# A hybrid decoder on one core: the mixer takes two heads with both token halves at a time

## The chip, the cores and the metric

The kernel runs on one core of a Trainium2 chip. The metric is device time in microseconds (us) of one execution. The engines are called as the profile calls them: PE multiplies matrices (PEld is its weight load), DVE and ACT work on tiles element by element, POOL does the same more slowly, and SP issues nearly all DMAs.

## The reference: what is computed

Two layers over 1024 tokens with 1024 channels, all in float32. Each layer is a mixer and an FFN (feed-forward network), each with a residual. The core of the mixer, cut:

```python
h = rms_norm(x, norm1_g)
proj = h @ w_in                      # 1024 x 3592: q, k, v, z (4 heads of 128 each), b, a, 3 x 512 for the short convolution
qkv = silu(causal_depthwise_conv(qkv, dn_conv_w))       # 4 taps
q, k = l2_normalize(q), l2_normalize(k)
beta = sigmoid(b_in); g = -exp(dn_a_log) * softplus(a_in + dn_dt_bias)
o_dn = chunk_gated_delta_rule(q, k, v, g, beta)          # a state of 128 x 128 per head, carried over the tokens
o_dn = rms(o_dn) * dn_norm_g * silu(z)
y = gate_b * causal_depthwise_conv(gate_c * hv, sc_conv_w)   # 3 taps
o_sc = rms(y) * sc_norm_g
x = x + concatenate([o_dn, o_sc]) @ w_out
x = x + (silu(h2 @ ffn_w_gate) * (h2 @ ffn_w_up)) @ ffn_w_down   # h2 = rms_norm(x, norm2_g), 2816 wide
```

The delta rule works chunk by chunk: inside a chunk a unit triangular matrix is inverted, between chunks the state S is carried on.

## The kernel before, in words

Tiles are 128 channels by 512 tokens, one half of the tokens; chunks are 128 tokens, so a half has four. Float32 is emulated: each operand is split into a rounded part `hi` and a rest `lo`, and a product is three matmuls, hi by hi, lo by hi and hi by lo (`mm3`, L176 to L181). One projection of 128 columns for one half is 8 times 3 matmuls of 128x512.

Weights come in tiles of 1024 by 128 (512 KB). `split_w` (L163) loads one, then `split_raw` casts it on ACT to `hi` (L172) and subtracts on DVE to get `lo` (L173). The input projection has 28 such tiles per layer, and the kernel works through the halves one after the other, so each tile is loaded and split twice per layer.

For one half the mixer runs: `make_h` (the normed input as hi/lo tiles), `ba` (beta and the decays of this half), then for each of four heads `proj_kvq` and `prep`; `invert` for the four heads; `chain` for the four heads; `sconv` for four groups, `sc_norm`, `zproj` and `gate`. One head with one half is called a unit below: three projections (72 matmuls of 128x512), each with `conv_silu` (L397: ACT copies the projection out of PSUM, DVE takes four taps at L408 and L410, ACT takes a tanh, DVE combines at L413), then 12 PE transposes (`ktok`, `qtok`, `vtok`), and 8 products `gk` and `gq` that are two passes each, 28 short PE records in all. `prep` computes row sums of squares (ACT L429, DVE L430), an inverse square root by ten small DVE operations (L151 to L160), decay rows `row` (ACT L464), and `U` and `A` on DVE, four operations of 128x128 each (L500).

`invert` is a loop of 31 steps on DVE over 32x32 blocks of all units at once, followed by merges on PE (`rp32`, `yp32`, `rp64`, `yp64`). `chain` carries the state: per chunk kS (PE), rr (DVE), TR (PE), vn (DVE), SU (PE), S (DVE), each needing the one before; each head is alone in its chain.

The second half's input x waits in DRAM (`xd`): `x_half1` puts it there during the first half of layer 0, and each mixer reads it back.

What sets the order: every engine runs its own instructions strictly in the order of the program, and a scheduler puts them into that order when the kernel is built. SP's queue is one such order. A pool gives a tile a fixed number of buffers: four for weight parts `whi` and `wlo`, three for the raw tiles. Where two tiles share a buffer, the later one waits for the last reader of the earlier one.

The FFN uses a scheme with 7 products instead of 8 for 2x2 blocks (`QORD`, P1 to P7); its operands go through the same rings and through buffers that the mixer also uses.

## Time and profile before

| what | us |
| --- | --- |
| three runs: median, lowest, highest | 2424.56, 2420.68, 2424.63 |
| the profiled execution, its own time | 2427.01 |
| its span, first to last instruction | 2425.3 |
| PE busy | 2344.0, 97% |
| DVE busy | 1821.2, 75% |
| ACT busy | 883.5, 36% |
| POOL busy | 720.5, 30% |

The span is what the engines show; 1.7 us of the execution lie around it. Busy shares are means over stages. The stretch from 0 to 500 us holds the mixer of layer 0, the one from 1200 to 1700 us that of layer 1, the rest are output projections and FFNs. A PE counted as busy may still be working below its pace, because one matmul's record overlaps the next; the number of records in a stretch says more.

### The profile page before, as it was taken

How to read it: one execution, taken by the hardware profiler on the slowest of the kernel's cores; microseconds unless marked ns; L12 is line 12 of the kernel's file. 1: busy time of each engine (PE TensorE's matmuls, PEld its weight loads, DVE VectorE, ACT ScalarE, POOL GpSimd, SP SyncE). 2: the span in 40 equal slices, each digit the busy share in tenths (PEclk: the TensorE clock that was granted, in tenths of full speed). 3: DMA queues.
4: the chain of work that ended last, by engine and by line, in shares of the span. 5: the costliest groups of instructions: out<-in, count | busy, mean ns of one | idle time of the engine just before them, and what ended most of it. 6: DMA issues, size and time to landing. Idle time of an engine off the chain costs nothing.

```text
span 2425.3 us, 32283 instructions
## 1 busy us (share of the span) xinstructions
PE 2344.0 (97%) x11530; PEld 1901.9 (78%) x11530; DVE 1821.2 (75%) x3607; ACT 883.5 (36%) x1389; POOL 720.5 (30%) x554
## 2 busy tenths in 40 slices
PE   8899999999999999999999999999999999999998
PEld 6787778886888888777777877878878888887777
DVE  7986996868566665889789779967686565568994
ACT  4522432434323223433344235334342323333334
POOL 2100100034543443456411000000444343434470
PEclk9999999999999999999999999999999999999999
DMA  7545343751432323745243354447433232346431
GB/s 224 137 107 150 97 112 89 208 180 61 126 113 87 109 94 105 239 143 150 96 127 98 95 148 107 111 120 220 126 91 115 86 113 91 117 138 218 139 119 70
DMA packets 423194, 307.74 MB, mean 127 GB/s; under 512 B 48463, under 2 KB 355961, under 8 KB 423033
## 3 DMA queue, kind: packets, MB, share of 16 engines
q1 hardware_dynamic: 423032, 305.69, 42.8%
q8 instruction: 90, 1.47, 0.3%
q14 instruction: 72, 0.58, 0.1%
HBM read 230.59 MB, written 75.04 MB: 126 GB/s over the span
## 4 chain that ended last, share of the span: by engine, by line
PE 74%; DVE 15%; DMA 6%; issue 2%; POOL 1%; ACT 1%; SPq 0%; POOLq 0%; ACTq 0%; DVEq 0%
PE P_g L180 6%; PE P_g L181 6%; PE P_g L179 6%; PE P_u L180 5%; PE P_u L179 5%; PE P_u L181 5%; PE P_d L180 3%; PE P_d L181 3%; PE P_d L179 3%; PE po L181 2%; PE po L179 2%; PE po L180 2%; DMA stP<-hs_P 1%; DMA row<-gd 1%; PE ps_bsc L181 1%
## 5 line engine op out<-in xcount | busy, mean ns | idle before, releaser
L180 PE MATMUL P_g<-lo_hP,hiP_g 128*128 128x512 f32 x616 | 241.7, 393 | 8.6 <-POOL lo_hP L760 4.7
L179 PE MATMUL P_g<-hi_hP,hiP_g 128*128 128x512 f32 x616 | 240.3, 391 | 1.2 <-ACT hi_hP L759 0.9
L180 PE MATMUL P_u<-lo_hP,hiP_u 128*128 128x512 f32 x616 | 240.9, 391 | 0.0
L181 PE MATMUL P_u<-hi_hP,loP_u 128*128 128x512 f32 x616 | 240.9, 391 | 0.0
L179 PE MATMUL P_u<-hi_hP,hiP_u 128*128 128x512 f32 x616 | 240.8, 391 | 0.0
L181 PE MATMUL P_g<-hi_hP,loP_g 128*128 128x512 f32 x616 | 239.7, 390 | 0.0
L180 PE MATMUL P_d<-lo_dP,hiP_d 128*128 128x512 f32 x504 | 199.5, 396 | 14.9 <-DVE lo_dP L760 13.4
L181 PE MATMUL P_d<-hi_dP,loP_d 128*128 128x512 f32 x504 | 196.7, 390 | 2.6 <-DVE loP_d L785 2.6
L179 PE MATMUL P_d<-hi_dP,hiP_d 128*128 128x512 f32 x504 | 196.4, 390 | 0.0
L180 PEld LDWEIGHTS P_g<-lo_hP,hiP_g 128*128 128x128 f32 x616 | 115.6, 188 | 39.7 <-DVE lo_hP L760 8.6
L784 ACT CAST hiP_g<-m_g 128x1024 fp32r<-128x1024 f32 (+1 forms) x66 | 60.1, 910 | 218.5 <-PE P_u L180 193.0
L760 POOL TENSOR_TENSOR lo_hP<-xh,hi_hP 128x512 fp32r<-128x512 f32 x24 | 38.0, 1614 | 336.2 <-ACT hi_hP L759 336.2
L179 PEld LDWEIGHTS P_g<-hi_hP,hiP_g 128*128 128x128 f32 x616 | 115.5, 188 | 27.3 <-ACT hi_hP L759 3.5
L179 PEld LDWEIGHTS P_u<-hi_hP,hiP_u 128*128 128x128 f32 x616 | 116.5, 189 | 24.4
L180 PEld LDWEIGHTS P_u<-lo_hP,hiP_u 128*128 128x128 f32 x616 | 116.4, 189 | 24.3
L181 PEld LDWEIGHTS P_u<-hi_hP,loP_u 128*128 128x128 f32 x616 | 116.3, 189 | 24.3
L181 PEld LDWEIGHTS P_g<-hi_hP,loP_g 128*128 128x128 f32 x616 | 115.7, 188 | 23.2
L1055 DVE TENSOR_TENSOR xT<-P_d,xT 128x512 f32<-128x512 f32 x192 | 124.9, 679 | 9.3 <-PE P_d L181 8.9
L180 PEld LDWEIGHTS P_d<-lo_dP,hiP_d 128*128 128x128 f32 x504 | 94.6, 188 | 46.5 <-DVE lo_dP L760 22.7
L181 PEld LDWEIGHTS P_d<-hi_dP,loP_d 128*128 128x128 f32 x504 | 94.7, 188 | 22.3 <-DVE loP_d L785 3.9
L179 PEld LDWEIGHTS P_d<-hi_dP,hiP_d 128*128 128x128 f32 x504 | 94.6, 188 | 19.8
L784 ACT CAST hiP_u<-m_u 128x1024 fp32r<-128x1024 f32 (+1 forms) x66 | 59.8, 909 | 136.9 <-PE P_g L180 68.2
(413 smaller groups left out, 6219.6 us busy)
## 6 DMA issues: line engine op xcount, KB each, us to landing
stP<-hs_P SPq DMA_DIRECT2D x126, 256.0 KB, 3.9
m_g<-in_ffn_w_gate_dram SPq DMA_DIRECT2D x44, 512.0 KB, 4.0
m_u<-in_ffn_w_up_dram SPq DMA_DIRECT2D x44, 512.0 KB, 4.6
hs_P<-t SPq DMA_DIRECT2D x72, 256.0 KB, 3.2
m_d<-in_ffn_w_down_dram SPq DMA_DIRECT2D x48, 384.0 KB, 4.0
hs_P<-c_u SPq DMA_DIRECT2D x70, 256.0 KB, 2.1
raw_o<-in_w_out_dram SPq DMA_DIRECT2D x32, 512.0 KB, 4.6
raw_k<-in_w_in_dram SPq DMA_DIRECT2D x16, 512.0 KB, 4.6
```

The costliest lines, as they stand in the source:

```text
L179: PE.matmul(ps, lhsT=w(k)[0], rhs=m(k)[0], start=k == 0, stop=False)
L180: PE.matmul(ps, lhsT=w(k)[0], rhs=m(k)[1], start=False, stop=False)
L181: PE.matmul(ps, lhsT=w(k)[1], rhs=m(k)[0], start=False, stop=k == n - 1)
L760: eng.tensor_tensor(res[1], src, res[0].bitcast(F32), ALU.subtract)
L784: S.copy(hi, src)
L1055: V.tensor_tensor(t, ps, t, ALU.add)
```

## The change

The loop is turned round: `for g in range(2)` takes two heads at a time and both halves of them, and a weight tile stays in its buffer for both halves. For that, the normed input of both halves must exist from the start: in layer 0 the second half of x is loaded and transposed in the prologue and in layer 1 `h1` is made where layer 0 ends. `ba` runs once for both halves. The statistics of a head are one piece of 16 columns (`head_stats`); sums of squares are taken by ACT with its accumulator, in four pieces; the first tap goes to ACT; the factor `c2` is put into `row` on POOL, so that U and A are one DVE operation each; `vn` is an ACT copy; two heads' chains alternate; the scaling of the short convolution moves to the load of the output projection's operands. Weight rings have three buffers instead of four. The matmuls of the projections stay as many as they were.

```diff
-NHB = 20
+NHB = 32
...
-    prep_ = ctx.enter_context(tc.tile_pool(name="prep", bufs=2))
+    prep_ = ctx.enter_context(tc.tile_pool(name="prep", bufs=3))
...
-        hi = ring.tile(list(raw.shape), F32R, tag="whi", name=f"hi_{name}")
-        lo = ring.tile(list(raw.shape), F32R, tag="wlo", name=f"lo_{name}")
+            hi = ring.tile(list(raw.shape), F32R, tag="whi", bufs=3, name=f"hi_{name}")
+            lo = ring.tile(list(raw.shape), F32R, tag="wlo", bufs=3, name=f"lo_{name}")
...
+            dma(xp[c][kk], x[0, HALF + c * P:HALF + (c + 1) * P, kk * HALF:(kk + 1) * HALF])
...
+            S.activation(sq, xp[c][kk], AF.Square, accum_out=s2x[:, c, kk:kk + 1])
+            ps = ps_(XTB[(c * 2 + kk) % 4], f"xtp1_{c}_{kk}", (P, 4, P))
+            for k in range(4):
+                PE.transpose(ps[:, k, :], xp[c][kk][:, k * P:(k + 1) * P], ident)
+            for k in range(4):
+                S.copy(xT[1][kk * 4 + k][:, c * P:(c + 1) * P], ps[:, k, :])
...
+    h1 = make_h(lambda k: xT[1][k], r, lambda k: c_norm1(0, k), ps_("fx", "bc_n1_0_1"), "n1_0_1")
+    for k in range(KD):
+        dma(xd[:, k, HALF:], xT[1][k])
...
-                V.tensor_scalar(y, pre[:, 0:HALF], c_conv(l, 0, chan), None, ALU.mult)
-                for j in range(1, 4):
+                S.activation(y, ps, AF.Copy, scale=c_conv(l, 3, chan))
...
+                for j in range(3):
                     V.scalar_tensor_tensor(y, pre[:, j:j + HALF], c_conv(l, j, chan), y, ALU.mult, ALU.add)
...
-                S.activation(sq, ps, AF.Square)
-                V.reduce_sum(dst, sq, axis=AX.X)
+                for c in range(4):
+                    S.activation(sq[:, c, :], ps[:, c, :], AF.Square, accum_out=dst[:, c:c + 1])
...
+                G.tensor_tensor(row, row, c2.unsqueeze(2).broadcast_to(sh4), ALU.mult)
...
-                    for c in range(4):
-                        V.scalar_tensor_tensor(dst[:, c, :], gp[:, c, :], sc[:, c:c + 1], row[:, c, :],
-                                               ALU.mult, ALU.mult)
+                    V.tensor_tensor(dst, gp, row, ALU.mult)
...
-                    V.tensor_scalar(vn, cp, pr["c1"][:, c:c + 1], None, ALU.mult)
+                        S.copy(vn, cp)
...
-                for g, y in enumerate(ys):
-                    rb = tmp("rb", f"rb_{nm}_{g}")
-                    dma(rb, dram_ap(rd[half], g * HALF, [[0, P], [1, HALF]]))
-                    V.tensor_tensor(y, y, rb, ALU.mult)
-                    dma(od[4 + g][half][:], y)
...
+            for g in range(2):
+                slots = {}
+                for hd in (2 * g, 2 * g + 1):
+                    if hd == 0:
+                        for ty in "kqv":
+                            kvq(hd, 0, ty)
+                        ba()
+                        for ty in "kq":
+                            kvq(hd, 1, ty)
+                    else:
+                        for ty in "kq":
+                            for half in range(2):
+                                kvq(hd, half, ty)
+                    head_stats(hd)
+                    for half in range(2):
+                        if (hd, half) != (0, 0):
+                            kvq(hd, half, "v")
+                        slots[hd, half] = len(slots)
+                        prep(hd, half, slots[hd, half])
+                invert(g)
+                for half in range(2):
+                    for hd in (2 * g, 2 * g + 1):
+                        merge(hd, half, slots[hd, half])
+                for half in range(2):
+                    chain(g, half)
+                if g == 0:
+                    for hd in range(2):
+                        w = split_w(wcols(1536 + hd * P), f"z{l}_{hd}")
+                        for half in range(2):
+                            zproj(hd, half, w)
...
+                    sconv(0)
+            for g in range(1, 4):
+                sconv(g)
+            sc_norm()
+            w = [split_w(wcols(1536 + hd * P), f"z{l}_{hd}") for hd in (2, 3)]
...
+                    if k >= 4:
+                        rb = sb("kdec", f"rb_{nm}_{k}")
+                        dma(rb, dram_ap(rd, ((k - 4) * NC + half * 4) * P, [[0, P], [1, HALF]]))
+                        V.tensor_tensor(ot, ot, rb, ALU.mult)
```

In the diff `V` is DVE, `S` is ACT and `G` is POOL. The new `head_stats` does for both halves of a head what `prep` did for one: the transposes of k and q, the sums of squares into 16 columns, one inverse square root, and the factors from it. In `chain` the loop over the two heads now lies inside the loop over the chunks.

Three places of the order. First SP's queue in the prologue of layer 0, where `wd` are zeroed DRAM buffers, `raw_q0_0_0` is the weight tile of q of head 0 for half 0. Before:

```order
L297 DMA wd0_119<-zero_406 128x4x128
L297 DMA wd1_120<-zero_406 128x4x128
L297 DMA wd2_121<-zero_406 128x4x128
L297 DMA wd3_122<-zero_406 128x4x128
L166 DMA raw_q0_0_0_572<-in_w_in_dram 128x8x128
L166 DMA raw_k0_1_0_725<-in_w_in_dram 128x8x128
L166 DMA raw_v0_1_0_770<-in_w_in_dram 128x8x128
L688 DMA xt1_0_970<-in_x_dram 128x1024
```

Now, with `raw_v0_0` the tile of v of head 0 and `xT1` the transposed tiles of the second half:

```order
L306 DMA xd_92<-xT1_0_243 128x512
L306 DMA xd_92<-xT1_1_244 128x512
L306 DMA xd_92<-xT1_2_245 128x512
L306 DMA xd_92<-xT1_3_246 128x512
L306 DMA xd_92<-xT1_4_247 128x512
L306 DMA xd_92<-xT1_5_248 128x512
L306 DMA xd_92<-xT1_6_249 128x512
L306 DMA xd_92<-xT1_7_250 128x512
L312 DMA wd3_121<-zero_597 128x4x128
L166 DMA raw_v0_0_688<-in_w_in_dram 128x8x128
L166 DMA raw_k0_1_1088<-in_w_in_dram 128x8x128
```

The eight writes of the second half's x to DRAM now stand ahead of the third weight tile; before, only zeros and the first half's writes did.

Second DVE in the projection stage of layer 0, before (end of the unit of head 0, into head 1):

```order
L479 TENSOR_TENSOR kdec_0_0_0_642<-kdec_0_0_0_642,kd_0_0_0_664 128x512
L500 SCALAR_TENSOR_TENSOR U_0_0_0_703<-gk_0_0_0_705,c2_0_0_0_663,row_0_0_0_617 128x128 x4
L500 SCALAR_TENSOR_TENSOR A_0_0_0_704<-gq_0_0_0_714,y_rk0_0_0_648,row_0_0_0_617 128x128 x4
L408 TENSOR_SCALAR y_v0_1_0_807<-pre_v0_1_0_803,cst1_88 128x512
L173 TENSOR_TENSOR lo_q0_2_0_1169<-raw_q0_2_0_1166,hi_q0_2_0_1168 128x1024
L410 SCALAR_TENSOR_TENSOR y_v0_1_0_807<-pre_v0_1_0_803,cst1_88,y_v0_1_0_807 128x512
L460 TENSOR_SCALAR ngl_0_2_0_1216<-gcum0_417 128x4
L173 TENSOR_TENSOR lo_k0_3_0_1322<-raw_k0_3_0_1319,hi_k0_3_0_1321 128x1024
L410 SCALAR_TENSOR_TENSOR y_v0_1_0_807<-pre_v0_1_0_803,cst1_88,y_v0_1_0_807 128x512
L406 COPY haloc1_0_847<-pre_q0_1_0_848 128x3
L408 TENSOR_SCALAR y_q0_1_0_852<-pre_q0_1_0_848,cst1_88 128x512
L410 SCALAR_TENSOR_TENSOR y_v0_1_0_807<-pre_v0_1_0_803,cst1_88,y_v0_1_0_807 128x512
```

Now, between head 2's two halves and head 3:

```order
L514 TENSOR_TENSOR U_0_2_0_2697<-gk_0_2_0_2699,row_0_2_0_2672 128x512
L501 TENSOR_TENSOR kdec_0_2_0_2565<-kdec_0_2_0_2565,kd_0_2_0_2677 128x512
L514 TENSOR_TENSOR A_0_2_0_2698<-gq_0_2_0_2705,row_0_2_0_2672 128x512
L424 SCALAR_TENSOR_TENSOR y_v0_2_1_2742<-pre_v0_2_1_2739,cst1_88,y_v0_2_1_2742 128x512 x3
L427 SCALAR_TENSOR_TENSOR vT_v0_2_1_2738<-pre_v0_2_1_2739,y_v0_2_1_2742 128x512
L492 TENSOR_TENSOR kd_0_2_1_2754<-row_0_2_1_2749,gcum0_608 128x4
L422 COPY halock3_0_2822<-pre_k0_3_0_2823 128x3
L417 COPY pre_k0_3_1_2860<-halock3_0_2822 128x3
L490 COPY gl_0_2_2627<-eta_0_2_1_2751 128x4
L495 TENSOR_TENSOR kd_0_2_1_2754<-kd_0_2_1_2754,c2_0_2_2619 128x4
L501 TENSOR_TENSOR kdec_0_2_1_2587<-kdec_0_2_1_2587,kd_0_2_1_2754 128x512
L504 SCALAR_TENSOR_TENSOR v2_0_2_1_2772<-vtok_0_2_1_2767,irk_0_2_2618 128x512
```

U and A are one operation instead of four, the first tap (L408) is gone, and a weight split (L176 there) is met half as often.

Third PE at the start of the first chain phase of layer 0, where TR, SU, op and kS belong to the chain, `rp32` and `yp32` to the merge of another unit, and `ps_` are projections of 128x512. Before:

```order
L589 MATMUL TR_0_0_0_0_1829<-v2_0_0_0_701,Y_0_0_0_1644 128x128
L180 MATMUL ps_z0_3_0_2734<-hlo_n1_0_0_2_362,hi_z0_3_0_2730 128x512
L181 MATMUL ps_z0_3_0_2734<-hhi_n1_0_0_2_361,lo_z0_3_0_2731 128x512
L179 MATMUL ps_z0_3_0_2734<-hhi_n1_0_0_3_367,hi_z0_3_0_2730 128x512
L594 MATMUL SU_0_0_0_0_1833<-vn_0_0_0_0_1831,kdec_0_0_0_642 128x128
L542 MATMUL rp32_0_1_0_1695<-X_0_1_0_1691,U_0_1_0_946 32x32
L603 MATMUL op_0_0_0_1828<-vn_0_0_0_0_1831,A_0_0_0_704 128x128
L180 MATMUL ps_z0_3_0_2734<-hlo_n1_0_0_3_368,hi_z0_3_0_2730 128x512
L542 MATMUL rp32_0_1_0_1695<-X_0_1_0_1691,U_0_1_0_946 32x32 x7
L181 MATMUL ps_z0_3_0_2734<-hhi_n1_0_0_3_367,lo_z0_3_0_2731 128x512
L179 MATMUL ps_z0_3_0_2734<-hhi_n1_0_0_4_373,hi_z0_3_0_2730 128x512
```

Now:

```order
L183 MATMUL ps_q0_2_0_2485<-hlo_n1_0_0_7_414,hi_q0_2_2481 128x512
L184 MATMUL ps_q0_2_0_2485<-hhi_n1_0_0_7_413,lo_q0_2_2482 128x512
L606 MATMUL TR_0_0_0_0_1747<-v2_0_0_0_993,Y_0_0_0_1561 128x128
L611 MATMUL SU_0_0_0_0_1751<-vn_0_0_0_0_1749,kdec_0_0_0_907 128x128
L621 MATMUL op_0_0_0_1745<-vn_0_0_0_0_1749,A_0_0_0_996 128x128
L601 MATMUL kS_0_0_0_1_1765<-S_0_0_0_0_1753,kT_k0_0_0_637 128x128
L620 MATMUL op_0_0_0_1745<-S_0_0_0_0_1753,qT_q0_0_0_675 128x128
L606 MATMUL TR_0_0_0_1_1769<-rr_0_0_0_1_1767,Y_0_0_0_1561 128x128
L557 MATMUL rp32_0_1_0_1612<-X_0_1_0_1608,U_0_1_0_1386 32x32 x8
L611 MATMUL SU_0_0_0_1_1773<-vn_0_0_0_1_1771,kdec_0_0_0_907 128x128
L621 MATMUL op_0_0_0_1745<-vn_0_0_0_1_1771,A_0_0_0_996 128x128
L565 MATMUL yp32_0_1_0_1624<-Y_0_1_0_1607,R32_0_1_0_1621 32x32 x2
```

Before, projection matmuls stood between the steps of the chain; now the first steps follow one another with only merges between them. Further on, 24 matmuls of `ps_q0_2_1` and the first of `ps_v0_2_0` stand in this phase.

## Rows read from the trace of the kernel before

**Rows 1.** The page, its first part: busy us, share of the span, instructions by engine

```profile
PE 2344.0 (97%) x11530; PEld 1901.9 (78%) x11530; DVE 1821.2 (75%) x3607; ACT 883.5 (36%) x1389; POOL 720.5 (30%) x554
```

**Rows 2.** 50 us of the FFN of layer 0: by engine busy us (xinstructions), PEclk, DMA share, GB/s

```profile
650.00:700.00 50.00, 50.00 (x222) 41.40 (x222) 30.88 (x35) 16.14 (x21) 18.33 (x14) 1.00 0.29 89
```

**Rows 3.** Timeline, head 3's chain in layer 0: start us, us, engine, line, operation

```profile
472.37 0.38 PE L584 MATMUL kS<-S,kT_k 128*128 128x128 f32 x2
...
472.59 0.39 PE L602 MATMUL op<-S,qT_q 128*128 128x128 f32 x2
...
475.58 0.38 PE L584 MATMUL kS<-S,kT_k 128*128 128x128 f32 x2
...
476.59 1.14 ACT L613 ACTIVATE on<-op,mo 128x128 f32<-128x128 f32 x4 [0.97 <-DVE mo L610]
```

**Rows 4.** The view of windows again, projection stages, layer 0, then layer 1

```profile
25.00:125.00 100.00, 92.05 (x451) 73.89 (x450) 86.80 (x263) 51.47 (x103) 13.46 (x23) 0.97 0.57 154
275.00:350.00 75.00, 71.27 (x360) 57.80 (x359) 73.78 (x247) 36.53 (x70) 8.83 (x8) 1.00 0.45 116
1200.00:1325.00 125.00, 119.44 (x583) 95.59 (x582) 114.00 (x327) 58.44 (x101) 22.72 (x27) 0.99 0.39 105
1460.00:1550.00 90.00, 85.81 (x436) 70.11 (x436) 87.67 (x286) 41.17 (x76) 8.85 (x8) 1.00 0.43 112
```

**Rows 5.** What PE waited for, 25 to 125 us: us in total, times, longest

```profile
PE vtok L438 <- DVE vT_v L413: 3.3, 2, 2.1
PE ktok L438 <- DVE kT_k L413: 2.0, 1, 2.0
```

**Rows 6.** DVE's groups, 26 to 125 us: xcount, busy us, mean ns, idle before

```profile
L410 DVE SCALAR_TENSOR_TENSOR y_v<-pre_v,cst,y_v 128x512 f32<-128x512 f32 x12 | 9.0, 747 | 0.1
...
L500 DVE SCALAR_TENSOR_TENSOR U<-gk,c,row 128x128 f32<-128x128 f32 x12 | 3.8, 342 | 0.0
...
L173 DVE TENSOR_TENSOR lo_k<-raw_k,hi_k 128x1024 fp32r<-128x1024 f32 x3 | 3.7, 1220 | 0.0
...
L430 DVE TENSOR_REDUCE sk<-sqk 128x4 f32<-128x512 f32 x4 | 2.7, 675 | 0.0
...
L408 DVE TENSOR_SCALAR y_k<-pre_k,cst 128x512 f32<-128x512 f32 x4 | 1.8, 458 | 0.0
...
L153 DVE TENSOR_SCALAR h_rk<-sk 128x4 f32<-128x4 f32 x3 | 0.5, 162 | 0.0
```

**Rows 7.** ACT's groups of the same stretch

```profile
L464 ACT ACTIVATE row<-row,ngl 128x128 f32<-128x128 f32 x15 | 4.8, 392 | 1.8 <-POOL row L461 1.8
...
L172 ACT CAST hi_v<-raw_v 128x1024 fp32r<-128x1024 f32 x3 | 3.1, 1047 | 2.1 <-DMA raw_v<-in_w_in_dram 2.0
...
L429 ACT ACTIVATE sqk<-kdec 128x512 f32<-128x512 f32 x4 | 2.5, 619 | 0.0
...
L691 ACT ACTIVATION_READ_ACCUMULATOR sq<-xt 128x1 f32 x8 | 1.5, 188 | 0.0
```

**Rows 8.** Timeline, one POOL operation and the DVE operation beside it

```profile
72.11 0.97 POOL L461 TENSOR_SCALAR_AFFINE_SELECT row<-row 128x512 f32<-128x512 f32 x1 [0.69 <-DVE kdx L458]
...
72.50 1.12 DVE L410 SCALAR_TENSOR_TENSOR y_q<-pre_q,cst,y_q 128x512 f32<-128x512 f32 x1
```

**Rows 9.** Timeline of the first 25 us: ACT, PE, SP's queue

```profile
16.86 0.20 ACT L293 ACTIVATE alog<-alog 128x8 f32<-128x8 f32 x1
...
19.57 0.59 PE L333 MATMUL ba_ps<-hhi_n,w_ba 128*16 128x512 f32 x1 [1.58 <-ACT hhi_n L214]
...
13.50 5.22 SPq L291 DMA_DIRECT2D xd<-xT  x8
```

**Rows 10.** DMA issues, 25 to 125 us: xcount, KB each, median us to landing

```profile
raw_q<-in_w_in_dram SPq DMA_DIRECT2D x4, 512.0 KB, 5.4
```

**Rows 11.** Windows of the first two chain phases of layer 0

```profile
202.90:267.20 64.30, 60.03 (x497) 46.80 (x497) 50.11 (x152) 24.42 (x53) 6.04 (x5) 0.97 0.52 140
421.40:477.30 55.90, 55.90 (x489) 45.27 (x489) 44.11 (x128) 25.57 (x48) 0.00 (x0) 1.00 0.70 192
```

More of the change, by code (lines that the diff above doesn't have):

```diff
@@ L125, in tile_hybrid @@
     od = [[dram.tile([P, HALF], F32, name=f"od{k}_{h}") for h in range(2)] for k in range(KD)]
-    gd = [dram.tile([16, P], F32, name=f"gd{h}") for h in range(2)]
+    gd = dram.tile([32, P], F32, name="gd")
     USZ = 129 * 128
@@ new lines, in chain @@
+                        if not first:
+                            PE.matmul(op[hd][:, c, :], lhsT=u["q"][:, cs], rhs=St, start=True, stop=False)
+                        PE.matmul(op[hd][:, c, :], lhsT=u["A"][:, c, :], rhs=vn, start=first, stop=True)
+                nm, h4 = f"{l}_{g}_{half}", slice(half * 4, half * 4 + 4)
+                mo = s8("mo", nm)
+                for i, hd in enumerate(hds):
+                    sumsq(op[hd], mo[:, i * 4:i * 4 + 4], f"o_{nm}_{i}")
+                    V.tensor_tensor(mo[:, i * 4:i * 4 + 4], mo[:, i * 4:i * 4 + 4], units[hd, half]["s2"][:, h4], ALU.mult)
```

602 lines of the change are left out of this document (285 added, 317 removed).

## The prediction

> **What bounds the kernel now.** I read the page first, then the windows, then PE's waits, and last the groups of DVE and ACT. On the page PE is busy 2344.0 of 2425.3 us [rows 1], so it looks as if nothing but matmul work could be taken away, and the change takes none. The windows correct this. In the FFN PE runs 222 matmuls of 128x512 in 50 us [rows 2], 0.225 us each. A short PE pass of 128x128 takes 0.11 us: in the timeline two of them start at 472.37 and the next pair at 472.59 [rows 3]. A unit of the mixer (one head, one half) has 72 of the first and 28 of the second: 72 x 0.225 + 28 x 0.11 = 19.3 us, or 0.193 us per record. Against this the projection stages are slow [rows 4]: 451 records should take 87.0 us and stand in 100, 360 take 69.5 of 75, 583 take 112.5 of 125, 436 take 84.1 of 90. So 13.0 + 5.5 + 12.5 + 5.9 = 36.9 us are lost there, though only 8.0 + 3.7 + 5.6 + 4.2 = 21.4 us of them show as idle PE. The rest is hidden in records that overlap less than they could. (Counting each window in the proportion 72 to 28 is an estimate; the other records there, x transposes and `ba`, are of the same two kinds.)
>
> The cause is to be seen in the same rows: DVE is busy 73.78 of 75 us in the window at 275 and 87.67 of 90 in the one at 1460. Per 100 PE records (one unit) that is 73.78 / 3.60 = 20.5 us of DVE, more than PE's 19.3. And PE's waits name it: the transposes of v and k wait for the convolution results vT and kT of DVE, 3.3 and 2.0 us between 25 and 125 [rows 5].
>
> **The change part by part.**
>
> DVE in a unit. Weight splits: three of 1.22 us [rows 6] per unit become three for two units, 1.83 us less. First taps: three of 0.458, 1.37 us less. Row sums: two of 0.675, 1.35 us less. U and A: eight of 0.342 become two of 128x512, which I price at 0.675 like the reduction of that shape, 1.39 us less. Two inverse square roots of ten small operations (0.162 each) per unit become one for two units: 15 x 0.162 = 2.43 us less. Together 8.4 us of 20.5. Records of an engine overlap a little, so the low end counts the first three alone: 4.6. DVE comes to 12.1 to 15.9 us per unit and is no longer the bound.
>
> ACT in a unit. It has 36.53 us in 3.60 units [rows 4], 10.1 each. Casts of 1.047 [rows 7] halve: -1.57. Two Squares of 0.619 go: -1.24. Three first taps of the same shape come: +1.86. Eight Squares of 128x128 at 0.392 with a read of the accumulator at 0.188 come: +4.64. Sum 13.8 us, still under 19.3. POOL gets one more operation of 128x512 per unit, on top of 8.83 / 3.60 = 2.5 us; the nearest row is its 0.97 [rows 8].
>
> So in the projection stages the unit falls from DVE's pace to PE's. What can be won is between all that is lost, 36.9, and what the two named waits explain: 5.3 of the 13.0 in the first window, which as a share of 36.9 is 15 us. What would stay in the second case is latency: the path from PSUM over ACT, three taps, tanh and the combination to the transposes does not get shorter. I take the middle, 26 us.
>
> Prologue of layer 0. The second half of x is now loaded, squared, transposed and copied there. ACT was free at 17.0 us [rows 9]. Before the last copy it now has 32 copies of 128x128 (four took 1.14 us [rows 3], so 9.1), eight Squares with reads (0.619 + 0.188, 6.5) and the eight casts of the first half's input (priced as 128x512, 0.619, 5.0): about 37.6 us. SP's queue holds the eight writes of those tiles to `xd`, then one zeroing write, then the load of v's first tile. Eight such writes took 5.22 us to issue [rows 9]; whether they go one by one as the tiles are done or all behind the last copy, the load leaves between 38.3 and 43, lands 5.4 us later [rows 10], and its cast adds 1.05: 45 to 49 us. PE's order has that v projection ahead of `ba` and of everything else. PE began the projections at 19.57 [rows 9] and until then has k and q of half 0 (48 x 0.225 = 10.8) and 32 transposes (3.5), done at about 34. It then stands idle for 11 to 15 us, of which 3.5 come back, since those transposes no longer stand in the stage behind. I take +9; the ends are 0 (the writes are out early) and +15.
>
> Chain phases. The two of layer 0 take 64.3 and 55.9 us now, with 4.3 and no us of idle PE [rows 11]. The order shows two changes: fewer projection matmuls stand between the steps (by the order some 115 in the first phase before, some 60 now, 12 us less cover), and two heads alternate, where before each head's chain ran by itself. A step of one head takes 3.21 us when little is in its way (kS at 472.37, the next at 475.58 [rows 3]); eight steps are 26 us. PE's own work in a phase is 60.0 - 115 x 0.225 = 34 us of chain and merge, plus 60 x 0.225 = 13.5, so 47.6: there are 22 us for the merges ahead of the last head's chain. vn goes from DVE to ACT; a 128x128 operation of ACT is 0.29 to 0.39 [rows 3, 7], of DVE 0.34 [rows 6], no difference by itself, but ACT's casts of 1.05 can stand ahead of it. I take 0; the ends are -8.6 (the idle 4.3 of the first phase goes in both layers, since DVE is freer and `make_h` has left the phase) and 8 x 1.05 = 8.4 in each of four phases, +34.
>
> Costed at nothing: the halved weight traffic (28 tiles x 512 KB x 2 layers), as the DMA share is 0.39 to 0.57 and no wait of PE names a weight tile in the stages; the ring of three weight buffers, since a split (1.05 + 1.22 = 2.3 us) fits beside one product of 12 matmuls (2.7 us) and PE is busy 50.00 of 50.00 in the FFN, at most one uncovered split at each of four passages between stages, +9; the second half's input at the start of layer 1, with 88 matmuls (19.8 us) of half 0 ahead of its first reader, against 8 x 0.75 + 4 x 0.68 = 8.7 us of DVE; the scaling in the output projection, where the 16 operations of about 0.68 us only move and z's projections (96 matmuls, 21.6 us) cover the statistics.
>
> One rule speaks against the new POOL work. While POOL worked 0.97 us from 72.11, a tap on DVE that takes 0.747 [rows 6] took 1.12 [rows 8]: DVE was held up 0.37. The Trainium skill, "Perfetto Trace Analysis", section "Optimizing Scalar/DVE Operations", says that GpSimd and DVE share a read port of SBUF, so that moving work between the two may not help; the trace agrees as far as this one row goes. By that rule the new row operation can take back up to its own length of DVE in every unit, and the time would move from the forecast towards rival A. The row alone shows a hold of 0.37 us for 0.97 us of POOL; it leaves DVE's unit under PE's, and so it counts here only in A's chance, which it raises a little.
>
> The sum: the profiled execution, 2427.0, less 26, plus 9, is 2410.0. It lies 2.4 above the median of the runs (2424.56), so I predict 2407.6, rounded 2408.
>
> **Rivals.**
>
> A, the gain is eaten (chance 0.16). Latency, not DVE's load, holds PE's transposes, so only 15 us are won, and the prologue costs its full 15: 2427.0 - 2.4 = 2424.6. For it: named waits are a minority of the lost time, ACT, which now takes both the copy and the first tap, lies on the same path, and POOL, which can hold DVE up [rows 8], has more to do. Against it: DVE had no free time at all at 275, so its queue is a delay of its own.
>
> B, slower (0.14). The chains lose their cover: with PE's order fixed, a late vn holds up both heads and the merges behind it. It decides from a step of about 4.2 us on, one cast more than 3.21; then the four phases cost up to 34, and with the projection gain at 26 and the prologue at 9 the time is 2441.6. With half of it the kernel would be level. For it: PE's order starts the first phase with steps and merges and no projection between. Against it: 47.6 us of PE work against 26 of steps.
>
> C, a larger gain (0.15). All 36.9 are won, the idle 8.6 of the chains too, and the writes in the prologue are out early: 2427.0 - 45.5 - 2.4 = 2379.
>
> **How the numbers follow.** The forecast has 0.55, with a range of its own of 2396 to 2417 (projections 20 to 33, prologue 5 to 14). C and the forecast give faster by over 0.2%, 0.70. About 0.2%, some 5 us, is what a measurement of this kernel can tell from no change. A gives no change but for a small part on the slow side: same 0.14. B with that part: slower 0.16. The range 2380 to 2434 takes in A, nearly all of C and the lower part of B.
>
> **What would show it.** Right: in the windows of the projection stages the records per 50 us rise towards 259 (50 / 0.193), DVE's share falls from 97 or 98% to about 60 to 75%, ACT's rises, and the waits of the transposes for vT and kT shrink; in the prologue PE waits ten us for the tile of v or for a sum of the second half. The FFN windows stay at 222 records in 50 us. Wrong: PE's waits in the projection stages stay as they are with DVE half free (A), or the chain phases show waits for vn or S of many us (B), or no wait in the prologue (C).

## The result and the profile after

The changed kernel takes 2539.26 us (median of 4 runs, 2534.03 to 2545.77) against 2424.36 us of the kernel before in the same session: a ratio of 1.0479, interval 1.0453 to 1.0505. It is slower by 115 us, and the forecast of 2408 us with its range to 2434 was wrong, in sign too. The profiled run took 2534.03 us, its span 2532.3 us.

The page of the kernel after, busy us, share of the span and instructions, answers to [rows 1]:

```profile
PE 2385.5 (94%) x11522; PEld 1935.4 (76%) x11522; DVE 1666.4 (66%) x2771; ACT 911.6 (36%) x1925; POOL 770.4 (30%) x570
```

DVE has 155 us less to do, as was meant. PE has 41.5 us more, with 8 records fewer, and its idle time rises from 81 to 147 us (span less busy). Read from the trace as the end of the last matmul of each stage, layer 0 / layer 1, in us:

| stage | before | after | difference |
|---|---|---|---|
| mixer and output projection | 551.6 / 524.1 | 593.7 / 558.8 | +42.1 / +34.7 |
| gate and up | 431.8 / 431.8 | 435.7 / 435.7 | +3.9 / +3.9 |
| down, in groups | 185.2 / 184.6 | 197.8 / 197.4 | +12.6 / +12.8 |
| last rows of down | 50.7 / 51.3 | 48.0 / 51.0 | -2.7 / -0.3 |

The differences sum to the 107 us between the two profiled executions (that of the kernel after was its fastest of four). Nearly three quarters of the loss lie in the mixers, the rest in the FFN. The windows of the kernel after (us; PE, PEld, DVE, ACT, POOL busy with records; granted clock; DMA share; GB/s) answer to [rows 4] and [rows 2]:

```profile
25.00:125.00 100.00, 85.23 (x400) 64.41 (x399) 70.00 (x152) 57.10 (x180) 19.99 (x19) 0.93 0.39 108
275.00:350.00 75.00, 63.06 (x303) 51.60 (x302) 51.51 (x108) 31.97 (x100) 13.64 (x14) 0.95 0.24 57
...
650.00:700.00 50.00, 50.00 (x222) 41.44 (x221) 32.28 (x36) 14.88 (x20) 25.18 (x18) 1.00 0.39 127
```

In the projection stages DVE fell to 70% as forecast, and PE did fewer records, not more: 400 in the first window where 451 stood, 303 in the second where 360 stood (the stages no longer begin at the same us, so this compares kinds of stretch, not the same work). The steady FFN kept its 222. What PE waited for in the whole kernel after (us in total, times, longest):

```profile
PE vtok L451 <- DVE vT_v L427: 21.9, 10, 4.6
PE qtok L451 <- DVE qT_q L427: 15.6, 4, 4.7
PE P_d L183 <- POOL lo_dP L770: 13.0, 10, 2.5
PE P_d L182 <- ACT hi_dP L769: 9.4, 6, 2.5
PE sp_sc L451 <- ACT sq_sc L446: 8.9, 4, 3.4
PE P_u L182 <- ACT hiP_u L794: 6.9, 2, 3.5
...
PE ps_v L182 <- ACT hi_v L175: 6.7, 1, 6.7
```

Of [rows 5] the wait for kT has gone; that for vT was 3.3 us in one stage there, and qT has come as new. One such wait can be followed through three engines (start, duration, operation, idle before and its releaser; layer 0, the second head). ACT:

```profile
104.73 0.69 ACT L420 ACTIVATE y_k<-ps_k,cst 128x512 f32<-128x512 f32 x1
107.21 0.63 ACT L489 ACTIVATE eta<-row 128x512 f32<-128x512 f32 x1 [1.78 <-DMA row<-gd]
...
109.30 1.28 ACT L499 ACTIVATE row<-row,ngl 128x128 f32<-128x128 f32 x4 [0.95 <-POOL row L496]
110.49 0.62 ACT L426 ACTIVATE pre_k<-y_k 128x512 f32<-128x512 f32 x1
111.01 0.56 ACT L418 COPY pre_q<-ps_q 128x512 f32<-128x512 f32 x1
```

DVE:

```profile
107.88 0.17 DVE L490 COPY gl<-eta 128x4 f32<-128x4 f32 x1 [1.66 <-ACT eta L489]
...
108.03 1.78 DVE L424 SCALAR_TENSOR_TENSOR y_k<-pre_k,cst,y_k 128x512 f32<-128x512 f32 x2
...
115.27 0.69 DVE L427 SCALAR_TENSOR_TENSOR qT_q<-pre_q,y_q 128x512 f32<-128x512 f32 x1 [0.76 <-ACT pre_q L426]
```

PE:

```profile
116.02 0.72 PE L451 MATMUL qtok<-ident,qT_q 128*128 128x128 f32 x4 [4.01 <-DVE qT_q L427]
...
116.96 0.63 PE L183 MATMUL ps_v<-hlo_n,hi_v 128*128 128x512 f32 x1
117.39 0.63 PE L184 MATMUL ps_v<-hhi_n,lo_v 128*128 128x512 f32 x1
...
119.93 0.39 PE L184 MATMUL ps_v<-hhi_n,lo_v 128*128 128x512 f32 x1
120.16 0.39 PE L182 MATMUL ps_v<-hhi_n,hi_v 128*128 128x512 f32 x1
```

The decay row of the other half comes by DMA into the one `row` tile, so its load cannot go ahead of the last use of the row before. ACT stands at `eta`, DVE at `gl` behind ACT, two taps of k behind `gl` on DVE, and the copy of q out of PSUM, behind all that, at 111.01. PE's transposes of q wait 4.01 us for it. Behind the wait the matmuls start 0.427 us apart, from 119.93 on 0.23.

### The profile page after: what moved, and what is told of

Same layout as the page of the kernel before. It is cut to its first block, busy times and chain, and to the rows that moved or that the text cites. A ratio compares the mean times of both kernels' runs of the same rounds, so it can differ in the third digit from the quotient of the medians.

```text
span 2532.3 us, 31892 instructions
## 1 busy us (share of the span) xinstructions
PE 2385.5 (94%) x11522; PEld 1935.4 (76%) x11522; DVE 1666.4 (66%) x2771; ACT 911.6 (36%) x1925; POOL 770.4 (30%) x570
## 4 chain that ended last, share of the span: by engine, by line
PE 70%; DVE 12%; issue 6%; DMA 5%; ACT 4%; POOL 2%; SPq 0%; POOLq 0%; ACTq 0%; DVEq 0%
PE P_g L183 5%; PE P_g L184 5%; PE P_g L182 5%; PE P_u L183 5%; PE P_u L182 5%; PE P_u L184 5%; PE P_d L183 3%; PE P_d L182 3%; PE P_d L184 3%; DMA row<-gd 2%; PE po L182 2%; PE po L183 2%; PE po L184 2%; PE ps_hsc L182 1%; PE ps_hsc L183 1%
## 5 line engine op out<-in xcount | busy, mean ns | idle before, releaser
L182 PE MATMUL P_d<-hi_dP,hiP_d 128*128 128x512 f32 x504 | 202.4, 403 | 11.6 <-ACT hi_dP L769 9.4
```

The lines of the kernel that those rows point to most:

```text
L182: PE.matmul(ps, lhsT=w(k)[0], rhs=m(k)[0], start=k == 0, stop=False)
```

## The experiments

All ratios are to the kernel before, run beside each kernel; two changed kernels are compared by their medians, also across sessions, in which the median of the kernel before lay between 2420.77 and 2424.36 us. Most edits also made the scheduler put PE's instructions into another order. What an edit gave is then the gain of the edit with its new order; the table behind e14 shows where it lies.

**e1, the kernel before with DVE relieved** as in the change (first tap and the sums to ACT), nothing else:

```diff
-                V.tensor_scalar(y, pre[:, 0:HALF], c_conv(l, 0, chan), None, ALU.mult)
+                S.activation(y, ps, AF.Copy, scale=c_conv(l, 3, chan))
-                S.activation(sq, ps, AF.Square)
-                V.reduce_sum(dst, sq, axis=AX.X)
+                for c in range(4):
+                    S.activation(sq[:, c, :], ps[:, c, :], AF.Square, accum_out=dst[:, c:c + 1])
```

> The kernel before, with two of the change's edits alone: the first tap of each convolution goes from DVE to ACT, and sums of squares are taken by ACT in four pieces with its accumulator, so DVE loses 1.37 + 1.35 us per unit and the loops stay as they were. Theory D (my prediction: DVE's load sets the pace of the projection stages): 16 units x about 2 us, 20 to 30 us faster than before, near 2398. Theory S (PE's fixed order puts each transpose a set number of matmuls behind its projection, and what counts is whether the path over ACT and DVE is done by then): within 8 us of before, or slower, since the order is built anew and transposes can move closer to their projections.

2445.08 us, 1.0085 [1.0070, 1.0100]: slower by 21 us by the ratio, 23 by the medians. In the window from 275 to 350 us DVE is busy 66.97 us in place of 73.78, and PE does 336 records in place of 360: with DVE no longer full the stage got slower. This move cannot tell DVE's load from ACT's, which it raises (e11 does that). PE waits more for vT (6.3 us in 6 before, whole kernel):

```profile
PE vtok L438 <- DVE vT_v L413: 15.6, 9, 2.7
```

**e2, the kernel before with fewer staging tiles** for the stored rows of the down projection:

```diff
-STG = ("th", "pre", "rb", "th", "pre", "k", "q")
+STG = ("th", "pre", "th", "pre")
```

> The kernel before, with one table altered: the tiles in which the FFN's stored hidden parts come back (STG) rotate over four buffers (th and pre) instead of seven names (th, pre, rb, th, pre, k, q). Theory F1 (the 13 us more of each down projection after the change come from the shorter rotation of these tiles, so loads come late and the cast waits for them): the two down stages get 8 to 13 us longer each, about 20 us in all, 2444. Theory F2 (they come from the weight ring of three instead of four): no change, 2424 within 5.

2436.70 us, 1.0052 [1.0034, 1.0070]: 14 us more by the medians, where theory F1 had some 20. The down stages grow by 8.2 and 9.4 us, to 193.4 and 194.0, as it said; the mixer of layer 1 and the last rows of layer 0 are 3 and 2 us shorter. Staging alone can cost two thirds of what the change lost in down.

**e3, the kernel after in another order of emission** (v ahead of `head_stats`, the odd head's k ahead of the even head's `prep`, one z projection and one short convolution earlier), so that more matmuls stand ahead of the late transposes.

```diff
+                    kvq(hd, 1, "v")
+                    if hd % 2 == 0:
+                        kvq(hd + 1, 1, "k")
```

> The changed kernel with another order in which the program is written, the same instructions: v of half 0 ahead of the head statistics, v of half 1 and the next head's k (or z of head 0, or the convolution group 1) ahead of the two prep calls. In PE's order q's transposes then stand 24 to 48 matmuls behind their projection instead of 20 to 24, v's 59 to 72 instead of 18 to 27. Theory S: the waits for vT and qT of 4 to 5 us go at all four places of each layer's odd heads and with them the slower matmuls behind each; 25 to 45 us faster than the changed kernel, about 2500. Theory E (work moved to ACT and POOL makes the path long): less than 10 us. Theory R (the single row tile holds ACT and DVE up): less than 10 us.

2537.27 us, 1.0462 [1.0439, 1.0485], the same as the kernel after, so theory S's 25 to 45 us did not come. The waits moved to k's transposes and to the start of the output projection:

```profile
PE po L182 <- ACT hhi_o L906: 15.0, 5, 7.0
PE ktok L451 <- ACT sqk L446: 13.9, 4, 3.6
```

**e4, two tiles for the decay row** (room taken from the state tiles):

```diff
-"row": 1, ... "St": 6}
+"row": 2, ... "St": 4}
```

> The changed kernel with two buffers for the decay rows tile instead of one (and four instead of six for the state, to make room). Theory R (ACT's exponential of the row waits for the row's DMA, and the copy of the next projection stands behind it in ACT's order, so the transposes come late): 15 to 30 us faster than the changed kernel, about 2515. Theory S: within 8 us of it, 2539.

2502.82 us, 1.0320 [1.0299, 1.0340]: 36 us back. The wait for qT is gone, that for vT is 16.4 us. ACT's wait for the load is not new: it is as long in the kernel before as in the kernel after. DVE's is three times as long. In turn, before, after and e4 (where ACT has no such wait left):

```profile
ACT eta L455 <- DMA row<-gd: 32.1, 15, 6.8
DVE kdx L458 <- DMA row<-gd: 4.3, 5, 1.8
```

```profile
ACT eta L489 <- DMA row<-gd: 31.2, 15, 3.4
DVE kd L492 <- DMA row<-gd: 14.4, 11, 2.5
```

```profile
DVE kd L492 <- DMA row<-gd: 3.5, 5, 1.1
```

So a wait of 31 us on ACT did little harm before and costs 36 us after (26 by the two profiled executions): it is what stands behind it in the queues that differs. In PE's order, as the traces have it, a median of 32 (q) and 43 (v) matmuls of 128x512 stood between a projection and its transposes before, and 24 and 20 do after. What this distance is worth e8 shows.

**e5 to e8, one edit each on top of e4.** e5 loads and splits v's first weight tile in the prologue; e6 puts the first tap and the sums back on DVE (e1's diff the other way round); e7 deepens the staging; e8 has e3's order without the moved short convolution.

```diff
-        for c0, name, eng in ((512, f"k{l}_0", G), (0, f"q{l}_0", G)):
+        for c0, name, eng in ((512, f"k{l}_0", G), (0, f"q{l}_0", G), (1024, f"v{l}_0", V)):
-STG = ("pre", "h", "pre", "h", "pre", "h")
+STG = ("pre", "h", "y", "pre", "h", "y", "pre", "h")
```

> The kernel after with two buffers for the row tile (2502.8 us in its own run), and with the v weight tile of layer 0's first head loaded and split in the prologue, beside k's and q's, on VectorE. Theory V (the v tile's late arrival holds the first stage; PE waits 6.7 us for ACT's hi_v there and the slower matmuls behind it add some): 5 to 9 us less than that run, so a ratio to the kernel before of 1.028 to 1.030, and layer 0's mixer alone is shorter. Rival (the prologue's other loads and the half-2 sum take the place of the wait): within 3 us of that run.

2499.08 us, 1.0321 [1.0293, 1.0350]: not to be told from e4 by its time. In its trace PE's wait of 6.7 us for `hi_v` is gone, and layer 0 reaches its first chain phase at 196.8 us, e4 at 205.3 and e7, with the same order up to there, at 203.3: theory V's size.

> The kernel after with two buffers for the row tile (2502.8 us), and with the first tap back on VectorE and the row sums of squares as one ACT Square of 512 and one VectorE reduce, in place of the ACT tap and four ACT Squares with a sum each, as the kernel before had it. Theory E (ACT's share of the unit's chain sets when the transposes can run, and VectorE at 66% has room): the waits of sp_sc for sq_sc (5.3 us) and of vtok for vT (16.4 us) shrink and the time falls by 10 to 20 us. Rival (VectorE's order is as tight as ACT's, so the chain only moves): within 5 us, with waits on DVE in place of those on ACT. A loss over 5 us would say that VectorE holds the chain now.

2468.61 us, 1.0193 [1.0170, 1.0215]: 34 us back, more than the theory asked for; 15 of them lie in the first chain phases, which the new order fills better (table behind e14). With four Squares and four reads a unit's sum costs ACT this (e4; mean ns of one, layer 0):

```profile
L446 ACT ACTIVATE sqk<-ktok 128x128 f32<-128x128 f32 x32 | 8.6, 303 | 0.0
...
L446 ACT ACTIVATION_READ_ACCUMULATOR sqk<-ktok 128x1 f32 x32 | 7.4, 233 | 0.0
```

and with one Square this (e6):

```profile
L445 ACT ACTIVATE sqk<-ktok 128x512 f32<-128x512 f32 x8 | 4.8, 604 | 3.0 <-DVE ss L446 2.3 <-DVE m_sc L446 0.8
```

that is 4 x 0.536 = 2.14 us of ACT's queue against 0.60. The same helper takes the sums of q, of the chain's output and of the short convolution, so the edit is larger than the two sums per unit that the prediction priced.

> The kernel after with two buffers for the row tile (2502.8 us), and with the staging of the stored rows as deep as the tiles that the mixer no longer needs at that time allow: the tuple STG is pre, h, y, pre, h, y, pre, h in place of pre, h, pre, h, pre, h. Theory F1 (the down projections' extra 13 us each come from fewer staging tiles; in the kernel before, taking them away cost 8 to 9 us for each): the two down stages get shorter by 3 to 7 us each and the rest stays, so 5 to 14 us in all. Rival (the loads are held by SP's queue, whatever the tiles): within 2 us.

2493.99 us, 1.0295 [1.0273, 1.0316]: 9 us back by the medians. The down stages, at 193.5 and 194.2, are 4.0 and 2.4 us shorter than in e4; the rest of the 9 is not theirs.

> The kernel after with two buffers for the row tile (2502.8 us), and with another order of emission in the mixer: v of a half ahead of its head_stats, the odd head's k ahead of the even head's prep, and the first z projection ahead of the last prep. Theory S (the in-order transposes stand too few matmuls behind the projection that feeds them, 18 to 27 in place of 31 to 48): the vtok waits (16.4 us) fall below 5 us, and the time falls by 10 to 20 us. Rival (the latency of the ACT and DVE chain only meets the next transposes, as it did with the single row tile, where the same kind of order moved the time by nothing): within 5 us, with waits at ktok or at the output projection's start in their place.

2502.66 us, 1.0330 [1.0308, 1.0353]: no gain. The vtok waits fell to 2.9 us and `sp_sc` waits 10.8 us for `sq_sc` instead. The time alone would say that the distance of the transposes is worth nothing, but the two traces say otherwise: the projection stages of both layers are 25 us shorter than in e4, as theory S has it, the first chain phases 16 and the last stretch 6 us longer. The projections that now keep the transposes apart are missing between the steps of the chain: 40 matmuls of 128x512 stand in a first chain phase, 65 in e4. That of layer 0 in e8, then in e4:

```profile
201.10:258.50 57.40, 51.30 (x419) 42.10 (x419) 25.69 (x76) 18.25 (x68) 0.20 (x2) 0.73 0.13 33
```

```profile
205.30:262.60 57.30, 54.24 (x444) 43.25 (x444) 27.94 (x79) 20.76 (x68) 0.20 (x2) 0.82 0.20 51
```

PE is idle 6.1 us in the one and 3.1 in the other, and the granted clock is lower. e3, with 40 in place of 52, lost its gain in the same way.

**e9, of e6 only the tap**, and **e10, e6's two edits with the single row tile.**

> The kernel after with two buffers for the row tile (2502.8 us), and of the two edits that together took 34 us off (2468.6 us) only the first tap back on VectorE; the four ACT Squares of 128 with their four reads of the sum stay. On ACT the four with their reads take 2.1 us for a unit and one Square of 512 takes 0.60, while the tap takes 0.70 there. Theory Q (the Squares' 1.5 us more in ACT's in-order queue is the larger part): the tap alone gives back 5 to 14 us, 2489 to 2498 us. Rival T (the tap, which stands between the copy of PSUM and the other taps, is the larger part): 2470 to 2485 us.

2479.63 us, 1.0228 [1.0213, 1.0244]: the tap is 23 us of the 34, the sums 11. Theory Q, which had the sums as the larger part, was wrong. In the traces 14.5 us of what the tap gave lie in the first chain phases, 10 in the projection stages.

> The kernel after with its single row tile, and with the first tap back on VectorE and the row sums as one Square and one reduce. If the single row tile and the two ACT edits are separate losses, this gives back the same 34 us as with two row tiles: 2505 us (2500 to 2510). If both act through the same wait (ACT's queue held at eta behind the row load), the loss left is that of the row tile or less: 2475 to 2495 us. If the row load's wait is the whole floor, little comes back: 2515 to 2530 us.

2498.59 us, 1.0305 [1.0290, 1.0321]: 41 us back with the single tile, 34 with two. The losses are separate in the main; the row tile is then worth 30 (2498.59 to 2468.61).

**e11, all four edits; e12, these in e8's order; e13, e11 with another staging tuple.**

```diff
-STG = ("pre", "h", "y", "pre", "h", "y", "pre", "h")
+STG = ("pre", "y", "h", "pre", "y", "pre", "h")
```

> The kernel after with two row tiles, the first tap and the sums on VectorE, the staging tuple of eight and v's first weight tile in the prologue: all four edits that gave something back. If they add up, 2468.6 - 8.8 - 3.7 = 2456 us (2450 to 2462), 1.013 of the kernel before. If the prologue and the stages of one layer share waits, up to 2466. To be below the kernel before (2424) it would need another 32 us, which no edit so far points to: about 8 us for each mixer with its output projection and some 7 to 10 us for each down stage should be left.

2456.86 us, 1.0133 [1.0109, 1.0156]: the edits add up. That they do so to the us is luck, since the 3.7 us taken for v's tile could not be told from nothing.

> The kernel with all four edits, and with the other order of emission (v ahead of head_stats, the odd head's k ahead of the even head's prep, the first z projection ahead of the last prep). With the ACT queue as it is in the kernel after this order moved the time by nothing (2502.7 to 2502.8 us). Theory S2 (the distance of the transposes from their projections matters only once ACT's queue is short): 5 to 15 us less than the kernel with the four edits. Rival (with ACT relieved the vtok and qtok waits are some 8 us in all, and the order only moves them): within 4 us.

2485.48 us, 1.0251 [1.0235, 1.0268]: 29 us worse, which neither theory had. Both mixers up to their last projection are longer (478.6 and 453.7 us against 461.2 and 438.9). The two chain phases of layer 0 in e12, then in e11:

```profile
200.30:256.60 56.30, 53.65 (x446) 43.35 (x446) 30.34 (x86) 16.52 (x48) 0.20 (x2) 0.85 0.13 33
380.40:428.80 48.40, 45.12 (x408) 36.35 (x408) 18.45 (x64) 11.51 (x39) 0.00 (x0) 0.86 0.20 56
```

```profile
189.00:237.80 48.80, 48.80 (x455) 38.88 (x455) 31.14 (x85) 17.42 (x49) 0.10 (x1) 1.00 0.24 60
365.10:410.60 45.50, 45.35 (x433) 35.55 (x433) 19.25 (x65) 12.04 (x41) 0.00 (x0) 1.00 0.21 59
```

The phases hold 67 and 32 matmuls of 128x512 in place of 74 and 60. PE is idle in them, its granted clock falls to 0.85 and 0.86, and together with layer 1's they cost 37 us more; the projection stages are 6 us shorter, as S2 has it.

> The kernel with all four edits (2456.9 us), and with the staging tuple pre, y, h, pre, y, pre, h in place of pre, h, y, pre, h, y, pre, h: of the 21 stored rows that a group stages, six then take an h tile, which with the group's 26 h tiles for operands fills the 32 of the pool exactly, so that a tile falls to the place that the group before has already used; with eight it falls to one that is used two places later. Theory F1 (the rest of the down stages' loss, 9.4 and 8.2 us against the kernel before, is staging tiles that wait for operands): the down stages fall by 4 to 8 us each, 2441 to 2449 us. Rival F2 (it is the weight ring of three, or the rhythm of the casts, whatever the staging): within 3 us, 2454 to 2460 us.

2447.78 us, 1.0109 [1.0084, 1.0134]: 9 us back by the medians, 6 by the ratios. The down stages are 189.2 and 191.2, that is 5.4 and 1.6 us less than in e11: F1 holds in layer 0, and in layer 1 the gain is below its 4 to 8.

**e14, the kernel after with matmuls in its longest waits**, every dependency left as it is:

```diff
+                for i in range(warm):
+                    PE.matmul(t.rearrange("p c i -> p (c i)"), lhsT=hs[0][i % KD][0][:, 0:P], rhs=hs[0][i % KD][0],
+                              start=True, stop=True)
...
-                    qtok = transposed(u["q"], f"qtok_{nm}_{half}", bank("ch0"))
+                    qtok = transposed(u["q"], f"qtok_{nm}_{half}", bank("ch0"), 14 * (hd % 2 == 1 and half == 0))
```

> The kernel after, with 14 matmuls of 128x512 more (3.2 us, their result is overwritten) ahead of the odd heads' transposes that wait longest (q of half 0, v of half 1, 4.0 to 5.0 us in each of the four projection stages). Nothing that the stages compute or wait for is changed. Theory C (a part of the loss is not the wait but the matmuls behind it: after the 4.0 us wait at 116 us eight of them start 0.427 us apart in place of 0.227, 1.6 us lost, and the granted clock stands at 0.93 there): 8 places of 1.6 us, some 13 us less than the kernel after (2539 us), so 2523 to 2530 us, and a higher granted clock in these stages. Rival L (the time behind a wait is given back by the next wait, since ACT's and DVE's chain sets the pace): within 4 us. If the 14 matmuls delay anything themselves: more than 2543 us.

2511.96 us, 1.0354 [1.0332, 1.0375]: 27 us less with 112 matmuls more. That is twice theory C's gain, but not in the places that it named. Behind the filled wait at 116 us the matmuls do start 0.23 us apart; yet the projection stages, with 25 us of added work, are 5 us longer than in the kernel after, since the next transposes wait in turn (`ktok` for ACT's `sqk`, 5.4 us in 4), as rival L has it. The gain lies in the first chain phases (17 us) and in the last stretch (10 us), which got no added matmul: PE's order was built anew there too, and 77 projection matmuls stand in a first chain phase in place of 52. Two windows out of that phase in the kernel after:

```profile
220.00:230.00 10.00, 7.53 (x80) 5.96 (x79) 3.31 (x9) 1.45 (x5) 0.00 (x0) 0.79 0.41 100
230.00:240.00 10.00, 10.00 (x80) 8.59 (x80) 3.34 (x10) 2.46 (x8) 0.00 (x0) 0.50 0.04 8
```

and of e14:

```profile
220.00:230.00 10.00, 10.00 (x107) 8.10 (x107) 5.11 (x15) 1.91 (x8) 0.00 (x0) 1.00 0.28 68
230.00:240.00 10.00, 10.00 (x101) 7.78 (x99) 6.79 (x24) 6.31 (x27) 0.10 (x1) 1.00 0.01 2
```

After a stretch in which PE was idle a quarter of the time, the kernel after does 80 records in 10 us at 0.50, the 1.2 GHz level; e14, not idle there, does 101 at 1.00. Summing 10 us x (1 - granted clock) over windows of 10 us through each trace gives 23 us in the kernel before, 75 after, 43 in e14 and 39 in e13. Some of that time PE had nothing to do, so the 52 us between before and after bound from above what the lower clock itself cost: under half of the 107 us between these two executions.

**Where the time lies.** The table cuts the mixers of both layers, with their output projections, into five stretches by PE's records: up to the first record of a merge or chain, that phase to its last record, and so on. Each number is the length of a stretch less 0.225 us [rows 2] for every projection matmul of 128x512 that starts in it (1760 or 1761 records in each layer), summed over the two layers, one execution of each kernel; e14's added matmuls are left in. The last two columns are of a first chain phase: such matmuls in it, and its granted clock in layer 0 / layer 1.

| kernel | first projection stage | first chain phase | second projection stage | second chain phase | last stretch | matmuls | clock |
|---|---|---|---|---|---|---|---|
| before | 84.7 | 77.3 | 50.4 | 60.7 | 10.4 | 116 | 0.97 / 0.97 |
| after | 112.8 | 82.0 | 63.4 | 62.5 | 39.6 | 52 | 0.84 / 0.93 |
| e1 | 85.3 | 79.8 | 62.1 | 63.4 | 11.4 | 108 | 0.95 / 0.97 |
| e4 | 106.2 | 79.5 | 51.0 | 64.1 | 33.4 | 65 | 0.82 / 0.93 |
| e8 | 86.9 | 95.8 | 44.8 | 63.8 | 39.1 | 40 | 0.73 / 0.76 |
| e9 | 97.1 | 65.0 | 50.4 | 62.8 | 33.9 | 74 | 1.00 / 1.00 |
| e6 | 95.9 | 64.2 | 46.1 | 64.0 | 30.0 | 74 | 1.00 / 1.00 |
| e11 | 84.9 | 64.2 | 45.8 | 64.0 | 30.8 | 74 | 1.00 / 1.00 |
| e12 | 80.0 | 82.4 | 44.5 | 82.4 | 34.8 | 67 | 0.85 / 0.85 |
| e13 | 87.2 | 64.2 | 46.2 | 64.0 | 28.9 | 74 | 1.00 / 1.00 |
| e14 | 118.1 | 65.2 | 63.2 | 62.8 | 29.7 | 77 | 1.00 / 1.00 |

In the kernels with the new loop the first chain phases cost 63 to 65 us wherever 74 or more matmuls stand in one, and 74 to 96 with 40 to 67 (e3, e5, e7 and e10, not in the table, included). No run changed this number alone, so that the missing cover is the reason is read from the rows and not tried. One order can also come out differently: e5 and e7 have e4's 65 matmuls and stand at 75.3 and 73.8 there.

## Why the prediction was wrong

**The step that failed** is "So in the projection stages the unit falls from DVE's pace to PE's", -26 us. In two of the four windows DVE was busy 98 and 97% of the time, in the others 87 and 91% [rows 4], and I read that as the bound. The projection stages (first and third column of the table) cost 135.1 us before and 176.2 after. e11 shows that relieving DVE wins nothing there: it keeps the weight splits halved, U and A in one operation each and half of the inverse square roots (1.83 + 1.39 + 2.43 = 5.65 of DVE's 20.5 us per unit, by the prediction's prices), has the taps and sums back on DVE, and its projection stages cost 130.7. The 4 us less are what 52 short records at 0.11 us come to that no longer stand in these stages. So DVE's load was not the bound, or another wait stood ready at the same price. What sets the pace is the way of one result from PSUM over ACT and DVE to PE's transposes, in three in-order queues. The prediction had this as the latency that "would stay", and it does not stay: the change made it longer. Of the 41 us the second row tile takes 19 away (e4), the tap and the sums 15 (e6), and with v's tile early as well nothing is left (e11).

**What ACT got** was priced well (eight Squares with reads 4.64 us; 8 x (0.326 + 0.257) = 4.66 in the trace after) and then judged by load: 13.8 of 19.3 us. By position it is dear. With the order that each brought, the sums cost 11 us and the taps 23 (e4, e9, e6). A tap takes 0.70 us on ACT and 0.458 on DVE [rows 6]. By the Trainium skill, "Trainium Architecture — The Big Picture", section "The five engines, in one table", simple arithmetic is what ScalarE is not for; the trace agrees in direction, and its 1.5 lies within the page's "up to about 3×".

**What the prediction never named** is the single `row` tile, 30 to 36 us (e4, e10). It was single before too, and the change put its load between one half's `prep` and the other's, ahead of the other unit's copies on ACT and taps on DVE. Rival A was right in kind (the waits of the transposes stay, with DVE a third free) and wrong in price: it let 15 us be won.

**POOL and DVE.** The row that I held against the new POOL work, 0.37 us lost beside 0.97 of POOL [rows 8], has a harsher successor in the kernel after:

```profile
99.15 2.63 DVE L424 SCALAR_TENSOR_TENSOR y_k<-pre_k,cst,y_k 128x512 f32<-128x512 f32 x2
102.90 0.74 DVE L424 SCALAR_TENSOR_TENSOR y_k<-pre_k,cst,y_k 128x512 f32<-128x512 f32 x1
```

```profile
98.06 1.72 POOL L515 TENSOR_TENSOR qT_q<-qT_q,eta 128x512 f32<-128x512 f32 x1
99.75 1.49 POOL L500 TENSOR_TENSOR row<-row,c 128x512 f32<-128x512 f32 x1
```

Two taps beside POOL's two operations take 2.63 us, where 1.48 would do, and POOL's new kind of operation takes 1.72 and 1.49 us here where I had 0.97. That is the port rule that the prediction cited from the Trainium skill ("Perfetto Trace Analysis", "Optimizing Scalar/DVE Operations"), and the trace agrees. The hold is not a fixed share: here and in [rows 8] the tap ends 0.54 us after the POOL operation beside it. What it cost in all was not measured by itself.

**The FFN, costed at +9 at most**, lost 33.2 in gate, up and down. I looked at the ring of weights and not at the staging tuple, which the diff shortens from seven tiles of five tags to six of two. In the kernel before the first fourteen loads leave one behind the other, in the kernel after two at a time, as their tiles come free, and PE waits for their casts. SP's queue, before and after:

```profile
966.14 15.17 SPq L983 DMA_DIRECT2D stP<-hs_P  x14
```

```profile
1011.48 1.97 SPq L997 DMA_DIRECT2D stP<-hs_P  x2
1014.37 2.67 SPq L997 DMA_DIRECT2D stP<-hs_P  x2
```

Staging alone costs 17.6 us in the kernel before (e2, both layers), and with better tuples, beside the other edits, e13 has 14.8 of the 25.4 in down back. The ring shows as one wait of 3.5 us for `hiP_u` at the start of each FFN, nearly all of the +3.9 there; that the ring of three causes it was argued and not tried.

**What was right.** The prologue: PE gets v's tile at 46.07 us, where I said 45 to 49, and waits 6.69 us for it. I had it idle for 11 to 15; it came to the wait at 39.4 us and not at about 34. The +9 for the whole term fits the 6.5 to 8.5 us that e5 gained there:

```profile
46.07 0.80 PE L182 MATMUL ps_v<-hhi_n,hi_v 128*128 128x512 f32 x1 [6.69 <-ACT hi_v L175]
```

The chain phases: the windows of the kernel after that answer to [rows 11] are

```profile
210.40:265.20 54.80, 51.40 (x434) 41.29 (x434) 26.72 (x77) 19.63 (x69) 0.20 (x2) 0.84 0.18 44
405.40:449.10 43.70, 43.56 (x429) 34.58 (x428) 17.21 (x62) 13.06 (x55) 0.00 (x0) 1.00 0.23 61
```

PE is idle 3.4 and 0.1 us there (4.3 and 0 before), and the four phases of the table cost 6.5 us more in all, which the term's range holds, so rival B did not happen at its price. Its mechanism, steps of the chain without projections between them, is there all the same: the first phase runs at a granted clock of 0.84, a cost that no wait shows and that I had not looked for, and it is the part that e6, e8, e12 and e14 move most.

**What had no term.** The last stretch, from the second chain phase to the end of the output projection, costs 29 us more, of which some 6 are short records that stood earlier in the kernel before. The end of the short convolution, z of two heads and the whole output projection now stand in it, and PE waits 12.6 us for the convolution's statistics (`sp_sc`) right behind the chain phase, with matmuls at the lower clock behind these waits.

**A slip in the sum.** The forecast's own range should end at 2418.6 (projections 20, prologue 14), not at 2417.

**What stays open.** e13 is the change with its tiles and ACT's work mended, and it is still 1.1% above the kernel before. Its mixers with output projections stand at 552.9 and 529.9 us against 551.6 and 524.1, gate and up at +3.9 each, down at +4.0 and +6.6. By the table it wins 13 us in the first chain phases and loses 18 in the last stretch, some 6 of them moved short records; PE is idle 4.1 and 3.6 us in the last stretches, 0.5 and 0 before. So the loop order, with half the weight traffic, gained nothing in the mixers in sum: there was no wait for weights that it could remove. That layer 1 keeps 5.8 us and layer 0 only 1.3 comes from the first projection stage; why was not settled. Whether an order exists that keeps the chain phases filled and the last stretch without waits was not tried.

## What to carry to other kernels

A busy engine is a bound only if the next engine in order waits for its throughput: before moving work off it, follow one result from PSUM to the matmul that reads it, and count what stands ahead of it in each in-order queue. When a loop order changes, list every tile with one buffer and every staging tuple, and ask whose load now stands between two uses. Price a wait of PE with the matmuls that run slower behind it. And where a scheduler orders anew with each edit, look in which stretch the time changed before the edit gets the credit: here the projections that an edit pulled out of the chain phases, or left in them, weighed nearly as much as the edit or more (e6, e8, e12, e14).

## What the hardware showed that was not expected

After a wait of 4.0 us the next matmuls started 0.427 us apart for 3 us, 1.6 us more. Behind short gaps it was the same: from 220 to 230 us PE was busy 7.53 of 10 us, in pieces, with the small matmuls of chain and merge, and over the next 10 us the granted clock was 0.50. 112 matmuls, 25 us of work, put into eight long waits made the stages that hold them only 5 us longer. Two taps of DVE beside POOL's 128x512 operations took 1.8 times their time, and ended 0.54 us after POOL did.
